# One more pair of the second feed-forward by seven products, with three pairs' weight sums, one unit's low part and a root moved to transfers

## The chip, the cores and the metric

The kernel runs on one core of a Trainium2 chip. Its engines each work through an instruction queue of their own, in order: TensorE (PE, with PEld for its weight loads), VectorE (DVE), ScalarE (ACT), GpSimd (POOL) and SyncE (SP), whose queue (SPq) only issues transfers here. POOL issues transfers too (POOLq), among them all those that add to what already stands at the destination. Semaphores let one engine wait for another. The metric is the device time of one execution in microseconds (us); less is better.

## What is computed

One layer for 512 prompt tokens and 8 single-token decoding sequences, 520 tokens in all, D_MODEL 1024, D_FF 2816. Cut to what matters here:

```python
def rmsnorm(x, g):
    return x * lax.rsqrt(jnp.mean(x * x, axis=-1, keepdims=True) + EPS) * g

def swiglu(x, w_gate, w_up, w_down):
    return (jax.nn.silu(x @ w_gate) * (x @ w_up)) @ w_down

def layer(x, ...):
    x = x + 0.5 * rmsnorm(swiglu(rmsnorm(x, ffn1_pre_g), *ffn1_w), ffn1_post_g)
    h = rmsnorm(x, mix_pre_g)
    ...        # o_r: retention, o_g: gated delta rule, both from h @ w_in
    y = (jax.nn.sigmoid(gate_r) * (o_r @ w_ret_branch)
         + jax.nn.sigmoid(gate_g) * (o_g @ w_gdn_branch))
    x = x + rmsnorm(y @ w_out, mix_post_g)
    return x + 0.5 * rmsnorm(swiglu(rmsnorm(x, ffn2_pre_g), *ffn2_w), ffn2_post_g)
```

All inputs and outputs are float32.

## The kernel before

**Operands.** Activations lie with channels on the 128 partitions and tokens along the free axis, in two halves of 260 tokens. To keep float32 precision every operand is split into a rounded high part and the low rest, and each product runs as three passes per 128 channels (`passes`, L409 to L416): high weights by high activations (L414), high weights by low activations (L415), low weights by high activations (L416). A weight tile arrives as `raw` (512 KB, L276 and L287, two buffers), ACT casts it to `whi` (L355) and DVE subtracts to get `wlo` (L356). A *unit* is one such tile; for 8 blocks of 128 channels, two halves and three passes it takes 48 matmuls.

**The feed-forwards.** Gate and up tiles come in pairs. `PLAIN` says how many pairs at the start are done plainly, as two units of 48 matmuls each: 3 in the first feed-forward, 4 in the second. The others (18 in the second) go by seven products in place of eight of half the depth: 7 products of 12 matmuls, 84 in all (`product7`, matmul tile `sv`). Each of the seven takes a 128 by 512 weight combination, which `split_seven` casts on ACT (L373) and subtracts on DVE (L374). Two combinations are sums that a DMA accumulates: `begin_pair` (L295 to L297) loads the first terms `s3`, `s1` and the plain part `a22` on SP, and `add_sums` (L307) issues two adding transfers on POOL. Two more are worked out on DVE: `s2` (L369) and `s4` (L377). The activation side has combinations too, made once by `token_factors` (L801 to L830): for each of four steps k, DVE works out `xd`, `ta` and twice `tb` (L816 to L820), ACT scales and casts (L815, L818, L824 `th`) and DVE subtracts `tl` twice (L825). The results of the seven products are combined in `pair`: ACT copies one product out of PSUM as `u` (L909), one as `q` (L912) and one as `u` again (L915).

**The way from the mixer to the second feed-forward.** The mixer's last products (`br`) give `branch` its input: DVE multiplies by the gate (L1281), POOL adds the other branch (`bt`, L1282), ACT casts `yh` (L1287) and DVE subtracts `yl` (L1288). Eight `wo` units (`down`, matmul tile `dn`) multiply these. Their results are squared on ACT (`s`, L528) and summed; at the third of them SP issues eight loads of the residual `x` (`load_x`, L743). `post` takes the inverse root of one half after the other (POOL's `rs` 87x3, L471), multiplies on DVE (L645), adds to the residual on POOL (L647) and splits the new residual into `xhl` (L517, L518). The first gate and up units of the second feed-forward (`first_units`, matmul tile `g`) start half by half on these; the first half's results are copied out of PSUM as `early` (L792). While they run, DVE adds the squares (`sq`, L549), PE sums them over channels (`ss`, L477), DVE writes the mean `ms` (L467), POOL takes the inverse root `rs` 87x6 (L471), PE spreads it over all partitions as `rb` (L483, 12 records) and ACT and DVE copy one half each (L573, L571). `hidden` then computes silu of the gate times up for the plain pairs: DVE `t` (L889), ACT `s` (L893), DVE `h` (L896).

**The order.** Every helper is a generator; `tick` runs between groups of matmuls and advances them, and a `yield n` puts the rest n ticks later. The `LATER` table adds or takes ticks at single places. So the code order on each engine's queue is fixed when the kernel is built. `self.rooted` becomes true when the second mean is there, and only then do `token_factors` of the second feed-forward and its `begin_pairs` start.

Of the kernel before, what the change touches and what calls it, by code (L numbers as in the profile page):

```python
# [7 lines left out]
F32 = mybir.dt.float32  # L8
F32R = mybir.dt.float32r
AF = mybir.ActivationFunctionType  # L10
ALU = mybir.AluOpType
# [22 lines left out]
PIECE_AT = [i * (HC - PW) // (PIECES - 1) for i in range(PIECES)]  # L34
# [8 lines left out]
PLAIN = {1: 3, 2: 4}  # L43
SPLIT_H = (8, 21)
LEAD = 3
GATE_COLS = 72
# [124 lines left out]
class Kernel:  # L171
    def __init__(self, ctx, tc, a):
# [34 lines left out]
        self.rooted = False  # L207
        self.ahead = 0
# [58 lines left out]
    def load_to(self, j):  # L267

        nc, a = self.nc, self.a
        while self.raw_next < min(self.group[min(j, len(self.unit_list))] + RAW_BUFS, self.group[-1]):  # L270
            u = self.unit_list[self.first_of[self.raw_next]]
            if u[0] == "seven":
                w, m = a[f"gu{u[1]}"], u[2]
                s1, s3, a22 = self.begun.pop((u[1], m), None) or self.begin_pair(u[1], m)
                t = self.raw.tile([P, KD, P], F32, tag="raw", name=self.name("raw"))
                nc.sync.dma_start(out=t, in_=w[2 * m])  # L276
                t = [t[:, 0:KH], s3, None, a22, t[:, KH:KD], s1, None]
# [64 lines left out]
    def split(self, j, parts):  # L342
# [15 lines left out]
    def split_seven(self, j):  # L358
# [8 lines left out]
        if i == s2:  # L367
# [5 lines left out]
        nc.scalar.copy(w[:, 0], t[i])  # L373
        nc.vector.tensor_tensor(w[:, 1], t[i], w[:, 0].bitcast(F32), ALU.subtract)  # L374
        if i == 4:
# [179 lines left out]
    def inverse_rms(self, acc, r, plus, held=False):  # L555
# [8 lines left out]
        if held:  # L564
            self.hold_sums = False
# [10 lines left out]
        for hf, (c0, n) in enumerate(HALVES):  # L576
            r[hf] = out[:, c0 : c0 + n]
        self.hold_sums = False
# [186 lines left out]
    def first_units(self, xs, name, groups):  # L765
# [4 lines left out]
        early = [self.slot("early") for _ in range(n // 2)]  # L770
        for hf, (c0, cols) in enumerate(HALVES):
            for group in groups:
# [12 lines left out]
                for j in group:  # L785
# [3 lines left out]
                    else:  # L789
# [10 lines left out]

    def token_factors(self, xs, r, gcol, F, f):  # L801

        nc = self.nc
        while len(xs[1]) < KD or f == 2 and not self.rooted:
            yield 0

        if f == 2:
            self.begin_pairs(f)
        tt, stt = nc.vector.tensor_tensor, nc.vector.scalar_tensor_tensor
        for k in range(KH):  # L810
# [9 lines left out]
            stt(out=tb[:, 1], in0=x21, scalar=g2, in1=tb[:, 0], op0=ALU.mult, op1=ALU.subtract)  # L820
            yield 1
# [329 lines left out]
    def mixer(self, xs, r, plus_next, x_from):  # L1151
# [98 lines left out]
        for out, g in ((RG, GR), (GZ, GG)):  # L1250
            for m in range(0, KD, 2):
# [4 lines left out]
                for z in range(2):  # L1256
                    ks = slice(z * H, (z + 1) * H)
                    ps = self.product([((hi[:, ks, :], lo[:, ks, :]), range(H))], ox, "br", z, BRANCH_HALVES)
                    self.spawn(self.branch(g, m + z, gate.pop((g, m + z)), ps, part, yx))
        return self.down(yx, (8,), self.vec[:, V_MPOST : V_MPOST + 8], V_G2PRE, 3, None, plus_next, x_from)  # L1260

    def branch(self, g, m, gate, ps, part, yx):
# [15 lines left out]
        for hf, (c0, n) in enumerate(BRANCH_HALVES):  # L1278
# [3 lines left out]
            nc.gpsimd.tensor_tensor(ts[hf], ts[hf], part[m][:, cs], ALU.add)  # L1282
        yield 3
# [752 lines left out]
```

## Time and profile before

| | |
|---|---|
| median of 3 runs | 1190.89 us (1189.58 to 1191.94) |
| profiled execution | 1189.49 us |
| its span in the profile | 1187.7 us, 1.8 us less than its time |
| granted TensorE clock | 0.999 |
| busy: DVE, ACT, POOL | 907.3, 602.6, 265.2 us |
| matmul and transpose records on PE | 9831 |
| transfers | 170.90 MB, 79178 packets |

Times inside the program are microseconds from the span's start. A timeline row gives the start, the length, the engine, line and operation, result and operands and the number of instructions; an arrow names a releaser: `[0.62 <-ACT yh L1287]` says that the engine stood idle for 0.62 us before this instruction, and that the idle time was ended by ACT's write of `yh` on line 1287. A view by windows gives, for a stretch of time, its length and then the busy time of PE, PEld, DVE, ACT and POOL with the number of instructions in brackets, the granted clock, the share of the DMA engines and the GB/s; asked for PE alone it gives the length, PE, the clock, share and GB/s. The mixer ends near 771 us, the `wo` units run until about 805, and the second feed-forward's first matmul of seven products stands a little after 870.

### The profile page before, as it was taken

To read this page: it belongs to the slowest core of one execution; us is meant where nothing else is said; L and a number is where in the kernel's file an instruction comes from. 1 tells how busy PE (TensorE), PEld (TensorE's weight loads), DVE (VectorE), ACT (ScalarE), POOL (GpSimd) and SP (SyncE) were. 2 spreads that over 40 slices of the span, in tenths; PEclk is the share of its full clock that TensorE was granted. 3 is DMA by queue.
4 is the path that set the end of the run, shared out by engine and by line. 5 is a ranking of instruction groups with operands and counts; after the bars stand their busy time and mean duration, and the time that the engine had idled before them with its cause. 6 is when DMAs were issued, how large, how long until landed. Compare 5 with 4: busy or idle time off the path is not lost. (4 is left out here: it accounts for less than half of the span.)

```text
span 1187.7 us, 25427 instructions
## 1 busy us (share of the span) xinstructions
PE 1172.0 (99%) x9831; PEld 1161.0 (98%) x9831; DVE 907.3 (76%) x1935; ACT 602.6 (51%) x1378; POOL 265.2 (22%) x477
## 2 busy tenths in 40 slices
PE   9999999999999999999999999999999999999998
PEld 8999999999999999999999999999999999999997
DVE  7988888777558788887677777746888888867555
ACT  7656666544336456313354774335555666644331
POOL 1111111000005248755551101404211111000000
PEclk9999999999999999999999999999999999999999
DMA  8777775233342533322367653242677777332334
GB/s 264 186 196 188 183 176 142 70 114 87 109 174 62 179 92 107 105 83 74 111 193 224 225 197 125 76 157 89 178 217 191 185 187 183 103 97 67 98 113 148
DMA packets 79178, 170.90 MB, mean 144 GB/s; under 512 B 17040, under 2 KB 18992, under 8 KB 79056
## 3 DMA queue, kind: packets, MB, share of 16 engines
q1 hardware_dynamic: 66768, 144.98, 38.1%
q0 software_dynamic: 12288, 24.29, 11.9%
q8 instruction: 77, 1.26, 0.4%
q14 instruction: 45, 0.37, 0.1%
HBM read 157.37 MB, written 11.86 MB: 142 GB/s over the span
## 5 line engine op out<-in xcount | busy, mean ns | idle before, releaser
L414 PE MATMUL p<-xhl,whi 128*128 128x260 f32 (+1 forms) x784 | 231.1, 295 | 0.0
L415 PE MATMUL p<-xhl,whi 128*128 128x260 f32 (+1 forms) x784 | 221.3, 282 | 0.1
L416 PE MATMUL p<-xhl,wlo 128*128 128x260 f32 (+1 forms) x784 | 221.2, 282 | 0.0
L356 DVE TENSOR_TENSOR wlo<-raw,whi 128x1024 fp32r<-128x1024 f32 (+2 forms) x111 | 132.9, 1202 | 50.1 <-ACT whi L355 48.4
L414 PE MATMUL sv<-th,w 128*128 128x260 f32 x592 | 167.6, 283 | 1.8 <-ACT q L912 1.8
L415 PE MATMUL sv<-tl,w 128*128 128x260 f32 x592 | 167.1, 282 | 0.0
L416 PE MATMUL sv<-th,w 128*128 128x260 f32 x592 | 167.1, 282 | 0.0
L415 PEld LDWEIGHTS p<-xhl,whi 128*128 128x128 f32 (+1 forms) x784 | 147.2, 188 | 0.7 <-DVE xhl L518 0.7
L414 PEld LDWEIGHTS p<-xhl,whi 128*128 128x128 f32 (+1 forms) x784 | 146.9, 187 | 0.9 <-DVE qk L1562 0.2
L416 PEld LDWEIGHTS p<-xhl,wlo 128*128 128x128 f32 (+1 forms) x784 | 147.0, 187 | 0.0
L307 POOL DMA_DIRECT2D s<-gu_in x74 | 65.0, 954 | 308.4 <-DMA s<-gu_in 156.1
L374 DVE TENSOR_TENSOR w<-s,w 128x512 fp32r<-128x512 f32 x148 | 101.6, 689 | 37.6 <-ACT w L373 36.7
L414 PE MATMUL dn<-hh,whi 128*128 128x260 f32 x448 | 127.0, 283 | 0.0
L415 PE MATMUL dn<-hl,whi 128*128 128x260 f32 x448 | 126.7, 283 | 0.0
L416 PE MATMUL dn<-hh,wlo 128*128 128x260 f32 x448 | 126.6, 283 | 0.0
L355 ACT CAST whi<-raw 128x1024 fp32r<-128x1024 f32 (+2 forms) x111 | 111.0, 1008 | 30.7 <-DMA raw<-dn_in 16.2
L414 PEld LDWEIGHTS sv<-th,w 128*128 128x128 f32 x592 | 111.3, 188 | 2.4 <-ACT q L912 2.2
L415 PEld LDWEIGHTS sv<-tl,w 128*128 128x128 f32 x592 | 111.5, 188 | 0.0
L416 PEld LDWEIGHTS sv<-th,w 128*128 128x128 f32 x592 | 111.4, 188 | 0.0
L373 ACT CAST w<-s 128x512 fp32r<-128x512 f32 x148 | 91.3, 618 | 34.1 <-DVE s L369 23.6
L471 POOL TENSOR_TENSOR rs<-ms,mhalf 87x3 f32<-87x3 f32 (+1 forms) x9 | 11.5, 1281 | 371.2 <-DVE ms L469 309.2
L416 PEld LDWEIGHTS dn<-hh,wlo 128*128 128x128 f32 x448 | 84.4, 188 | 0.0
(436 smaller groups left out, 3444.3 us busy)
## 6 DMA issues: line engine op xcount, KB each, us to landing
raw<-win_in SPq DMA_DIRECT2D x49, 512.0 KB, 3.6
raw<-gu_in SPq DMA_DIRECT2D x48, 512.0 KB, 5.2
s<-gu_in SPq DMA_DIRECT2D x74, 256.0 KB, 5.7
s<-gu_in POOLq DMA_DIRECT2D x74, 256.0 KB, 5.3
raw<-dn_in SPq DMA_DIRECT2D x32, 448.0 KB, 3.4
a<-gu_in SPq DMA_DIRECT2D x37, 256.0 KB, 5.8
x<-x SPq DMA_DIRECT2D x32, 260.0 KB, 5.5
raw<-dn_in SPq DMA_DIRECT2D x16, 512.0 KB, 3.6
```

The lines of the kernel that those rows point to most:

```text
L307: self.nc.gpsimd.dma_start(out=out, in_=term, accum_op=ALU.add)
L355: self.nc.scalar.copy(hi[:, ks], t[:, ks])
L356: self.nc.vector.tensor_tensor(lo[:, ks], t[:, ks], hi[:, ks].bitcast(F32), ALU.subtract)
L373: nc.scalar.copy(w[:, 0], t[i])
L374: nc.vector.tensor_tensor(w[:, 1], t[i], w[:, 0].bitcast(F32), ALU.subtract)
L414: mm(ps, hi[:, k, :], xh, start=first, stop=False, skip_group_check=more)
L415: mm(ps, hi[:, k, :], xl, start=False, stop=False, skip_group_check=more)
L416: mm(ps, lo[:, k, :], xh, start=False, stop=last, skip_group_check=more)
L471: self.nc.gpsimd.tensor_tensor(r[0:PW], m[0:PW], self.mhalf[0:PW].to_broadcast([PW, n]), ALU.pow)
```

## The change

`PLAIN[2]` goes from 4 to 3, so the second feed-forward does 19 pairs by seven products. The first three of these (pairs 3, 4, 5, `WHOLE`) get all four weight sums by transfers: `begin_whole` loads five terms per pair on SP, and `whole_pairs` issues seven adding transfers per pair on POOL, 21 in all, in three rounds (12, 6, 3) after the mixer's last branch. `s2` and `s4` of these pairs are no longer worked out on DVE; as the sums have no negative terms, `s2` is negated in its cast on ACT and in its low part on DVE. One plain unit (5; the table lists 6 and 7 too, which no longer exist) gets its low part without DVE: ACT writes the negated, rounded tile into `wlo` and the cast into `whi`, and a transfer on POOL adds the raw tile from DRAM to `wlo`. The last inverse root is written to DRAM by SP and read back in four broadcast loads (`root_rows`) in place of the `rb` matmuls and copies; with this the three pieces start at tokens 0, 87 and 173. The first units' results are copied out of PSUM for both halves. The first step of the second `token_factors` no longer waits for the mean. The last branch is added on DVE and goes on one tick earlier.

```diff
-PIECE_AT = [i * (HC - PW) // (PIECES - 1) for i in range(PIECES)]
+PIECE_AT = [min(i * PW, HC - PW) for i in range(PIECES)]
...
-PLAIN = {1: 3, 2: 4}
+PLAIN = {1: 3, 2: 3}
+LOW_BY_DMA = {'gu2': (5, 6, 7)}
+WHOLE = 3
...
@@ split
+        kind, m, k0, k1 = self.unit_list[j]
+        if m in LOW_BY_DMA.get(kind, ()):
+            self.nc.scalar.activation(lo, t, AF.Copy, scale=-1.0)
+            self.nc.scalar.copy(hi, t)
+            self.nc.gpsimd.dma_start(out=lo, in_=self.a[kind][m, :, k0:k1, :], accum_op=ALU.add)
+            return
@@ split_seven
+        whole = t[7]
-        if i == s2:
+        if i == s2 and not whole:
             t[s2] = self.slot("s2", (P, KH, P))
...
-        nc.scalar.copy(w[:, 0], t[i])
-        nc.vector.tensor_tensor(w[:, 1], t[i], w[:, 0].bitcast(F32), ALU.subtract)
-        if i == 4:
+        if whole and i == s2:
+            nc.scalar.activation(w[:, 0], t[i], AF.Copy, scale=-1.0)
+            nc.vector.scalar_tensor_tensor(
+                out=w[:, 1], in0=t[i], scalar=-1.0, in1=w[:, 0].bitcast(F32), op0=ALU.mult, op1=ALU.subtract
+            )
+        else:
+            nc.scalar.copy(w[:, 0], t[i])
+            nc.vector.tensor_tensor(w[:, 1], t[i], w[:, 0].bitcast(F32), ALU.subtract)
+        if i == 4 and not whole:
             t[s4] = self.slot("s4", (P, KH, P))
@@ inverse_rms
-        if held:
-            self.hold_sums = False
+        if plus is not None and not held:
+            yield from self.root_rows(s, r)
+            return
+    def root_rows(self, s, r):
+        nc = self.nc
+        n = PIECES * PW
+        yield 2
+        d = self.dram.tile([2 * n], F32, name=self.name("root"))
+        nc.sync.dma_start(out=d.rearrange("(c p) -> p c", p=PW), in_=s[0:PW])
+        yield 3
+        out = self.wk.tile([P, TOK], F32, tag="rb", name=self.name("rb"), bufs=1)
...
+                nc.sync.dma_start(
+                    out=out[:, c0 + t0 : c0 + to], in_=d[hf * n + at : hf * n + at + to - t0].unsqueeze(0).to_broadcast([P, to - t0])
+                )
+        yield 6
@@ first_units
-        early = [self.slot("early") for _ in range(n // 2)]
+        both = name == "g"
+        early = [[self.slot("early") for _ in range(n // 2)] for _ in range(1 + both)]
...
+                if both and hf:
+                    self.prefetch(True, 1)
+                for j in group:
+                    if both or not hf:
                         rows = slice(0, ws[j][0].shape[2])
-                        banks[j][0] = early[j // 2][rows, j % 2 * HC : j % 2 * HC + cols]
-                        self.nc.scalar.copy(banks[j][0], ps[j][rows])
+                        banks[j][hf] = early[hf][j // 2][rows, j % 2 * HC : j % 2 * HC + cols]
+                        self.nc.scalar.copy(banks[j][hf], ps[j][rows])
...
+    def begin_whole(self, f, m, later):
+        dma, w = self.nc.sync.dma_start, self.a[f"gu{f}"]
+        s1, s3, a22, s2, s4 = (self.slot(x, (P, KH, P)) for x in ("s1", "s3", "a22", "s2", "s4"))
+        a11, a12, a21, a4 = (w[2 * m + i, :, k : k + KH] for i in range(2) for k in (0, KH))
+        for out, term in ((s3, a11), (s1, a21), (s2, a11), (s4, a12), (a22, a4)):
+            dma(out=out, in_=term)
+        for out, term in ((s3, a21), (s1, a4), (s2, a21), (s4, a11)):
+            later[0].append((out, term))
+        later[1] += [(s2, a4), (s4, a21)]
+        later[2].append((s4, a4))
+        self.begun[f, m] = s1, s3, a22, s2, s4
+
+    def whole_pairs(self, f):
+        later = [[], [], []]
+        for m in range(PLAIN[f], PLAIN[f] + WHOLE):
+            self.begin_whole(f, m, later)
+            yield 6
+        while not self.joined:
+            yield 0
+        for terms in later:
+            for out, term in terms:
+                self.nc.gpsimd.dma_start(out=out, in_=term, accum_op=ALU.add)
+                yield 1
+            yield 2
...
@@ token_factors
-        while len(xs[1]) < KD or f == 2 and not self.rooted:
+        while len(xs[1]) < KD:
             yield 0
-        if f == 2:
-            self.begin_pairs(f)
...
             stt(out=tb[:, 1], in0=x21, scalar=g2, in1=tb[:, 0], op0=ALU.mult, op1=ALU.subtract)
+            while f == 2 and not self.rooted:
+                yield 0
             yield 1
@@ mixer
+            if out == GZ:
+                self.spawn(self.whole_pairs(2))
...
+        self.joined = True
@@ branch
-            nc.gpsimd.tensor_tensor(ts[hf], ts[hf], part[m][:, cs], ALU.add)
-        yield 3
+            eng = nc.vector if m == KD - 1 else nc.gpsimd
+            eng.tensor_tensor(ts[hf], ts[hf], part[m][:, cs], ALU.add)
+        yield 3 if m < KD - 1 else 2
```

The first place is POOL's queue between the mixer's last additions (`bt`) and the first half's inverse root (`rs` 87x3), before:

```order
L1282 TENSOR_TENSOR bt_10984<-bt_10984,yr_10668 128x256
L1282 TENSOR_TENSOR bt_10984<-bt_10984,yr_10668 128x264
L471 TENSOR_TENSOR rs_11431<-ms_11429,mhalf 87x3
L647 TENSOR_TENSOR x_11099<-x_11099,t_11448 128x260
```

and after, where eight rows stand for the 21 additions: the four of pair 3's first round, its two of the second, and the last round's first and last (a number behind `s_` names one sum):

```order
L1357 TENSOR_TENSOR bt_10969<-bt_10969,yr_10633 128x264
...
L868 DMA s_1820_10663<-gu_in 128x512
L868 DMA s_1819_10662<-gu_in 128x512
L868 DMA s_1822_10665<-gu_in 128x512
L868 DMA s_1823_10666<-gu_in 128x512
...
L868 DMA s_1833_10723<-gu_in 128x512
L868 DMA s_1834_10724<-gu_in 128x512
...
L868 DMA s_1823_10666<-gu_in 128x512
...
L868 DMA s_1849_10791<-gu_in 128x512
L489 TENSOR_TENSOR rs_11482<-ms_11480,mhalf 87x3
```

POOL's last two `bt` additions have left its queue (DVE makes them now), and 21 adding transfers stand between the branch and the inverse root.

The second place is DVE's queue behind the last `xhl` of the residual, before:

```order
L549 TENSOR_TENSOR sq_11496<-sq_11496,sq_11503 128x520
L356 TENSOR_TENSOR wlo_11875<-raw_11601,whi_11874 128x1024
L467 TENSOR_SCALAR ms_11895<-ss_11888 87x6
L561 TENSOR_SCALAR plus_27_155<-ms_11895 87x6
L816 TENSOR_TENSOR xd_11914<-x_11099,x_11103 128x260
L817 SCALAR_TENSOR_TENSOR ta_11912<-x_11103,vec,xd_11914 128x260
L819 SCALAR_TENSOR_TENSOR tb_11913<-x_11099,vec,ta_11912 128x260
L820 SCALAR_TENSOR_TENSOR tb_11913<-x_11101,vec,tb_11913 128x260
```

and after:

```order
L536 SCALAR_TENSOR_TENSOR xhl_11836<-x_11150,vec,xhl_11836 128x260
L885 TENSOR_TENSOR xd_11841<-x_11143,x_11147 128x260
L886 SCALAR_TENSOR_TENSOR ta_11839<-x_11147,vec,xd_11841 128x260
L888 SCALAR_TENSOR_TENSOR tb_11840<-x_11143,vec,ta_11839 128x260
L889 SCALAR_TENSOR_TENSOR tb_11840<-x_11145,vec,tb_11840 128x260
L567 TENSOR_TENSOR sq_11547<-sq_11547,sq_11548 128x520
...
L367 TENSOR_TENSOR wlo_11887<-raw_11654,whi_11886 128x1024
L485 TENSOR_SCALAR ms_11968<-ss_11961 87x6
```

The four operations of `token_factors`' first step have moved from behind the mean to ahead of the seven sums of squares and of unit 4's `wlo`.

The third place is ACT's queue at the first pairs by seven products, where `u` (first product out of PSUM) and `q` (another) are copied and `s` is the silu of a plain pair, before:

```order
L893 ACTIVATE s_12173<-t_12163 128x260
L893 ACTIVATE s_12174<-t_12164 128x260
L373 CAST w_2085_12223<-s_2011_11900 128x512
L373 CAST w_2090_12234<-raw_12060 128x512
L373 CAST w_2093_12289<-s_2015_11907 128x512
L373 CAST w_2094_12292<-s_2077_12160 128x512
L909 COPY u_12301<-sv_12282 128x260
L373 CAST w_2098_12318<-s_2097_12316 128x512
L912 COPY q_12321<-sv_12303 128x260
```

and after:

```order
L391 CAST w_2073_12139<-raw_11949 128x512
L964 ACTIVATE s_12143<-t_12109 128x260
L964 ACTIVATE s_12144<-t_12110 128x260
L964 ACTIVATE s_12168<-t_12157 128x260
L964 ACTIVATE s_12169<-t_12158 128x260
L391 CAST w_2083_12189<-s_1831_10721 128x512
L391 CAST w_2084_12192<-s_1823_10666 128x512
L980 COPY u_12203<-sv_12182 128x260
L386 ACTIVATE w_2087_12219<-s_1833_10723 128x512
L983 COPY q_12222<-sv_12205 128x260
```

Before, one silu pair and four casts stand ahead of the first `u` copy here; after, two silu pairs stand together, the second (`s_12168`, `s_12169`) with two casts between it and the copy.

More of the change, by code (lines that the diff above doesn't have):

```diff
@@ L207, in __init__ @@
         self.rooted = False
+        self.joined = False
         self.ahead = 0
@@ L273, in load_to @@
                 w, m = a[f"gu{u[1]}"], u[2]
-                s1, s3, a22 = self.begun.pop((u[1], m), None) or self.begin_pair(u[1], m)
+                s1, s3, a22, *both = self.begun.pop((u[1], m), None) or self.begin_pair(u[1], m)
                 t = self.raw.tile([P, KD, P], F32, tag="raw", name=self.name("raw"))
                 nc.sync.dma_start(out=t, in_=w[2 * m])
-                t = [t[:, 0:KH], s3, None, a22, t[:, KH:KD], s1, None]
+                t = [t[:, 0:KH], s3, None, a22, t[:, KH:KD], s1, None, bool(both)]
+                if both:
+                    t[2], t[6] = both
             elif u[0] == "down7":
@@ L563, in inverse_rms @@
         self.hold = held
-        if held:
-            self.hold_sums = False
+        if plus is not None and not held:
+            yield from self.root_rows(s, r)
+            return
+        self.hold_sums = False
         yield 4
@@ L577, in inverse_rms @@
             r[hf] = out[:, c0 : c0 + n]
+        self.hold_sums = False
+    def root_rows(self, s, r):
[6 more added lines that the diff above has]
+        out = self.wk.tile([P, TOK], F32, tag="rb", name=self.name("rb"), bufs=1)
+        last = PIECE_AT[-1]
+        for hf, (c0, _) in enumerate(HALVES):
+            for at, to in ((0, last), (n - PW, HC)):
+                t0 = to - (PW if at else last)
+                nc.sync.dma_start(
+                    out=out[:, c0 + t0 : c0 + to], in_=d[hf * n + at : hf * n + at + to - t0].unsqueeze(0).to_broadcast([P, to - t0])
+                )
+        yield 6
+        for hf, (c0, cols) in enumerate(HALVES):
+            r[hf] = out[:, c0 : c0 + cols]
         self.hold_sums = False
@@ L788, in first_units @@
                         self.release()
-                    else:
+                if both and hf:
+                    self.prefetch(True, 1)
+                for j in group:
+                    if both or not hf:
                         rows = slice(0, ws[j][0].shape[2])
-                        banks[j][0] = early[j // 2][rows, j % 2 * HC : j % 2 * HC + cols]
-                        self.nc.scalar.copy(banks[j][0], ps[j][rows])
+                        banks[j][hf] = early[hf][j // 2][rows, j % 2 * HC : j % 2 * HC + cols]
+                        self.nc.scalar.copy(banks[j][hf], ps[j][rows])
                 if hf:
```

## The prediction

> **What bounds the kernel now.** I read the busy table first, then PE alone in a quiet stretch, then PE's waits, and last the timelines around the places that the change touches.
>
> ```profile
> PE 1172.0 (99%) x9831; PEld 1161.0 (98%) x9831; DVE 907.3 (76%) x1935; ACT 602.6 (51%) x1378; POOL 265.2 (22%) x477
> ```
>
> PE is busy all the time, so time goes only where matmuls go or where PE stands. The stretch from 900 to 1000 us (length, PE busy and matmuls, clock, DMA share, GB/s) gives the price of one:
>
> ```profile
> 900.00:1000.00 100.00, 100.00 (x837) 1.00 0.75 187
> ```
>
> 100 us for 837 matmuls at full clock is 0.1195 us each. One pair by seven products in place of two plain units is 84 in place of 96 matmuls: 1.43 us less. The waits of PE (total, times, longest) say what else there is to win near the change:
>
> ```profile
> PE rb L483 <- POOL rs L471: 1.9, 3, 1.0
> PE u L414 <- DVE h L896: 0.5, 1, 0.5
> ```
>
> None is long, and the whole kernel has little idle PE; a change that shortens work on DVE or ACT pays only through such waits. What it can cost is any new wait.
>
> **Part A, the last branch on DVE.** Before, POOL's last additions and PE's wait are:
>
> ```profile
> 772.09 1.44 POOL L1282 TENSOR_TENSOR bt<-bt,yr 128x256 f32<-128x256 f32 x2 [1.33 <-DVE bt L1281]
> 774.05 0.39 PE L414 MATMUL dn<-yh,whi 128*128 128x260 f32 x1 [0.62 <-ACT yh L1287]
> ```
>
> POOL needs 1.44 us for two; DVE's additions of 260 columns take 0.42 (below), so the operand is ready about 0.6 us sooner. Low parts come from DVE right behind, so I take 0.45 of the 0.62: **-0.45 us**.
>
> **Part B, the 21 adding transfers.** POOL is free from 771, and the additions stand in its queue from there. Two stretches show what such transfers do to SP's. From 853 to 859 both queues have work (packets, MB, share of 16 engines); from 864 to 869 SP's alone:
>
> ```profile
> q0 software_dynamic: 381, 0.70, 63.4%
> q1 hardware_dynamic: 365, 0.93, 43.9%
> ```
>
> ```profile
> q1 hardware_dynamic: 1020, 1.90, 99.7%
> ```
>
> Together they fill the engines (107%), and they pass equal numbers of packets: 63 and 61 a us. Alone SP passes 204 a us. So a queue of additions cuts SP to under a third. Between 843 and 876 six additions went through q0 (the last number below is the median time to landing):
>
> ```profile
> q0 software_dynamic: 764, 1.40, 24.2%
> s<-gu_in POOLq DMA_DIRECT2D x6, 256.0 KB, 8.1
> ```
>
> That is 128 packets each, one for a partition, and 24.2% of 33 us over six is 1.33 us of all engines each. So 21 of them are 2688 packets, 42 us at that rate: they reach from 771 to about 809, since before 778 SP has little. Beside them, from the issues on SP:
>
> ```profile
> 778.03 0.33 SPq L287 DMA_DIRECT2D raw<-wo_in  x1
> 778.41 3.75 SPq L743 DMA_DIRECT2D x<-x  x8
> 784.01 0.33 SPq L287 DMA_DIRECT2D raw<-wo_in  x1
> ```
>
> ```profile
> q1 hardware_dynamic: 2018, 5.28, 45.1%
> x<-x SPq DMA_DIRECT2D x8, 260.0 KB, 5.1
> raw<-wo_in SPq DMA_DIRECT2D x3, 512.0 KB, 3.7
> ```
>
> (The second fence is 771 to 805.) The eight `x` loads are 8 x 128 = 1024 packets and a raw weight tile 128. In SP's order the seventh `wo` tile, issued at 784.01, stands behind them: from 778.03 that is 128 + 1024 + 128 = 1280 packets, 21.1 us at 61. The time from the last packet to landing I bound by two small transfers of the stretch 619 to 630, and take the middle, 2.8:
>
> ```profile
> s<-pack SPq DMA_DIRECT2D x8, 8.0 KB, 3.9
> pack<-s SPq DMA_DIRECT2D x4, 16.0 KB, 1.7
> ```
>
> With -0.45 from part A it lands at 778.0 + 21.1 + 2.8 - 0.45 = 801.4, where before such a tile landed 3.7 us (median) after its issue. It is needed here:
>
> ```profile
> 792.93 1.04 ACT L355 CAST whi<-raw 128x1024 fp32r<-128x1024 f32 x1
> 801.07 0.28 PE L414 MATMUL dn<-yh,whi 128*128 128x260 f32 x1
> ```
>
> PE takes the tile at 801.07 - 0.45 = 800.6; its low part, wanted two matmuls later, needs 1.04 us on ACT, 1.22 on DVE (as `wlo` at 840.54 below) and handovers of 0.2, so the tile must land by 798.4. It is **3.0 us** late. Next, the first gate tile can be issued only when this split is done, near 803.7 (before 795.43, when the buffer came free), lands in 3.5 to 6 us, and ACT casts it ahead of the last squares of `dn`. These end between 808.9 and 811.4, against 810.0 on a schedule shifted by 3.0 - 0.45: 0 to 1.4 us. Additions still run, so I take **1.3 us**. B is +4.3.
>
> ```profile
> 809.16 0.86 POOL L471 TENSOR_TENSOR rs<-ms,mhalf 87x3 f32<-87x3 f32 x1 [35.62 <-DVE ms L467]
> ```
>
> The additions stand ahead of this root on POOL; shifted by 4.3 - 0.45 it is wanted at 813, after their end at 809, so it costs nothing. The cover is 4 us. B's bounds: nothing, if the tile still lands by 798.4; 7 to 8, if additions are a fifth slower than q0's row.
>
> [...]
>
> **Part C, from unit 4 to the pairs by seven.** The stretch from unit 4's first matmul to the fourth `sv` product is 32.70 us before:
>
> ```profile
> 842.70:875.40 32.70, 30.83 (x255) 1.00 0.90 272
> ```
>
> After, it holds units 4 and 5 and three `sv` products, and the extra pair stands later. I follow DVE, whose rows are:
>
> ```profile
> 833.62 1.91 DVE L518 SCALAR_TENSOR_TENSOR xhl<-x,vec,xhl 128x260 fp32r<-128x260 f32 x3 [0.32 <-ACT xhl L517]
> 835.45 5.17 DVE L549 TENSOR_TENSOR sq<-sq,sq 128x520 f32<-128x520 f32 x7
> 840.54 1.22 DVE L356 TENSOR_TENSOR wlo<-raw,whi 128x1024 fp32r<-128x1024 f32 x1
> 844.48 0.16 DVE L467 TENSOR_SCALAR ms<-ss 87x6 f32<-87x6 f32 x1 [2.72 <-PE ss L477]
> 850.20 0.42 DVE L816 TENSOR_TENSOR xd<-x,x 128x260 f32<-128x260 f32 x1
> 851.98 0.42 DVE L571 COPY rb<-rb 128x260 f32<-128x260 f32 x1
> 852.32 0.69 DVE L825 TENSOR_TENSOR tl<-ta,th 128x520 fp32r<-128x520 f32 x1
> 853.54 0.42 DVE L889 TENSOR_TENSOR t<-early,rb 128x260 f32<-128x260 f32 x1
> 860.66 0.68 DVE L374 TENSOR_TENSOR w<-raw,w 128x512 fp32r<-128x512 f32 x1
> 861.26 0.68 DVE L374 TENSOR_TENSOR w<-s,w 128x512 fp32r<-128x512 f32 x1
> ```
>
> (All times here are before B's shift, which moves the whole part alike, with A's -0.45.)
> 1. Unit 4's `wlo`: DVE is free at 835.0; four operations of step 0 (850.20 to 851.98, 1.78), the sums 5.09, `wlo` 1.22: ready at 843.1. PE wants it two matmuls after 842.25: it waits **0.6**.
> 2. Unit 4 ran from 842.70 to 850.79 with the spreading matmuls in it; without them 8.09 - 1.25 = **6.84**, by these rows:
>
> ```profile
> 847.28 1.47 PE L483 MATMUL rb<-cst,rs 87*128 87x87 f32 x12
> 848.53 0.37 PE L414 MATMUL g<-xhl,whi 128*128 128x260 f32 x1
> 850.67 0.28 PE L416 MATMUL g<-xhl,wlo 128*128 128x260 f32 x1
> ```
>
> 3. Unit 5: 48 x 0.1195 = **5.74**, ending at 855.4. Its low part comes from the POOL transfer of 512 KB, issued near 837.5 and wanted near 849: the 8.1 us above for 256 KB and 1.33 for as much again end at 847, so it is covered.
> 4. The first `sv` wants the low part of its weights. DVE: `ms` at 844.7, 0.27 for it and its neighbour, two `tl` 1.22, three steps of 1.78 + 1.22 + 0.17 waiting on ACT, two `t` 0.68, the low part 0.60: 857.0. PE waits **1.4** with the handover. The root read through DRAM is covered: `rs` ends near 846.6, two small transfers of 1.7 to 3.9 each make 850 to 854.4, wanted at 855.7.
> 5. Three `sv` products, 12 x 0.1195 each: **4.29**.
> 6. Before the third, its PSUM bank must be freed by ACT's first `u` copy. Ahead of that, on ACT, stand four silus and two casts, and the last two silus wait for DVE's second `t` pair behind seven low parts (7 x 0.605), two `h` and two `t` (0.68 each): 856.4 + 4.2 + 1.4 = 862.0, then on ACT 0.65 + 1.05 + 0.2 to 863.9:
>
> ```profile
> 870.02 0.76 ACT L893 ACTIVATE s<-t 128x260 f32<-128x260 f32 x2 [1.87 <-DVE t L889]
> 871.71 1.14 ACT L373 CAST w<-s 128x512 fp32r<-128x512 f32 x2
> 872.75 0.36 ACT L909 COPY u<-sv 128x260 f32<-128x260 f32 x1
> ```
>
> PE is ready at 859.7: it waits **4.1**. Nothing in this stretch before waited so long; there the copy ran one silu pair later.
>
> The sum is 23.0 in place of 32.70, so -9.7; the extra pair later adds 84 x 0.1195 = +10.04. **C is +0.35**: the 1.43 us of matmuls, the 1.25 of spreading and about two of small waits are eaten by waits 1, 4 and 6.
>
> Other edits I cost at nothing. The four more `early` copies run where ACT is idle (8.53 us ahead of L818):
>
> ```profile
> 845.21 0.51 ACT L818 ACTIVATE ta<-xd,vec 128x260 f32<-128x260 f32 x1 [8.53 <-DVE xd L816]
> ```
>
> Without that gap they would cost 4 x 0.4. The 15 early loads (3.9 MB, some 10 us at the 1.90 MB in 5 us above) are spread among the first `wo` tiles, over 10 us ahead of the first addition; I take nothing. The removed `s2`, `s4` save DVE time that PE doesn't wait for. The pieces at 0, 87, 173 keep twelve `ss` matmuls.
>
> **Sum.** A -0.45, B +4.3, C +0.35: +4.2. The profiled execution takes 1189.49 (span 1187.7, 1.8 around it), so 1193.7; it lies 1.40 below the median of 1190.89. On the median: 1195.1, which I round to **1195.2**.
>
> **The rivals.**
> - *Transfers hidden* (not slower): the seventh `wo` tile lands by 798.4. It decides whether SP keeps at least 1280 packets in 18 us, 71 a us, beside the additions. Then B is nothing and A + C = -0.1: 1190.8. For it: additions wait for each other in rounds two and three, and POOL issues them 1.3 to 1.5 us apart, so there may be gaps; against it: three additions in 6 us already held SP to 61. [...]
> - *Transfers hidden, and no wait for the copy*: as above, and ACT's `u` copy comes in time since DVE takes silu's input earlier than I order it. Without the 4.1 us: 1186.7. Against it: both queues are in order and stand so.
> - *Additions hold the root*: if each takes a fifth longer than q0's row, the last is done near 819, 6 us after the root is wanted. POOL's `rs` then starts late, DVE's `t` behind it and PE's first gate unit: 1200.4 or so. For it: the 8.1 us of the six additions above, against the 5 or 6 us that round two and three would like.
>
> **How the numbers follow.** Chances: forecast 0.60 (1192.5 to 1199, from B's bounds), transfers hidden 0.24 (1189 to 1192.5), no copy wait 0.08, root held 0.08. A measurement of this kernel tells 0.2%, 2.4 us, from no change. Faster (under 1188.5): the third case and a tail of the second, 0.10. Same: most of the second and the forecast's lower edge, 0.22. Slower: 0.68. The range from 1189.5 to 1200 leaves out the third case, half the fourth and tails, 0.2 in all.
>
> **What would show it.** Part B: PE's `dn` waiting for `wlo` or `whi` near 800 with a releaser ACT or DVE behind a late raw tile, and `x` loads landing after 12 us or more in place of 5.1. Root: a POOL row of `rs` 87x3 whose releaser is POOL's own queue means the fourth case. Part C: waits of PE on `g` (0.6), the first `sv` on DVE's low part (1.4) and on ACT's `u` (4.1). If `dn` doesn't wait, B is wrong; if `sv` doesn't wait for `u`, step 6 is wrong; if the rows in the 900 to 1000 stretch hold fewer matmuls than 837, the extra pair has put a new wait into the steady part, which I haven't priced.

## The result and the profile after

The kernel after takes 1205.47 us (median of 4 runs, 1205.02 to 1206.33), the kernel before 1191.41 us (4 runs, 1189.58 to 1192.23): ratio 1.0121, 95% interval 1.0103 to 1.0139. It is slower by 14 us, where the prediction said 4. The profiled execution took 1205.02 us, its span 1203.3, at a granted clock of 0.994 in place of 0.999.

The busy table and the longest waits of PE, from the page and the waits of the kernel after (waited for, total, times, longest):

```profile
PE 1176.9 (98%) x9807; PEld 1164.7 (97%) x9807; DVE 907.6 (75%) x1939; ACT 608.2 (51%) x1390; POOL 281.0 (23%) x493
```

```profile
PE dn L432 <- ACT whi L366: 6.1, 1, 6.1
PE sv L434 <- DVE w L392: 3.5, 1, 3.5
PE sv L432 <- ACT u L980: 2.4, 1, 2.4
```

The three waits are the ones that the prediction named, at 3.0, 1.4 and 4.1 us (`dn` is a product of the `wo` units, `sv` one of the products by seven). PE has fewer matmuls than before and yet a longer busy time. Where that comes from shows in a view by windows (PE alone: length, busy, clock, DMA share, GB/s):

```profile
790.00:800.00 10.00, 10.00 (x86) 1.00 1.10 262
...
805.00:810.00 5.00, 2.31 (x9) 0.56 1.13 234
...
870.00:875.00 5.00, 4.18 (x22) 0.66 0.29 56
875.00:880.00 5.00, 3.46 (x19) 0.73 1.04 393
...
900.00:1000.00 100.00, 100.00 (x834) 1.00 0.73 182
```

Behind each of the three waits the granted clock drops; the kernel before reads 1.00 over 600 to 900. From 900 to 1000 PE is busy for all 100 us and waits for nothing, as before. That 834 records stand there and not 837 is thus no new wait of the extra pair, which the prediction had made a sign of being wrong. The timeline of PE shows it matmul by matmul:

```profile
800.87 0.28 PE L434 MATMUL dn<-yh,wlo 128*128 128x260 f32 x1
807.23 0.58 PE L432 MATMUL dn<-yh,whi 128*128 128x260 f32 x1 [6.08 <-ACT whi L366]
807.61 0.42 PE L433 MATMUL dn<-yl,whi 128*128 128x260 f32 x1
808.49 0.58 PE L434 MATMUL dn<-yh,wlo 128*128 128x260 f32 x1 [0.46 <-DVE wlo L367]
808.87 0.42 PE L432 MATMUL dn<-yh,whi 128*128 128x260 f32 x1
809.09 0.42 PE L433 MATMUL dn<-yl,whi 128*128 128x260 f32 x1
...
812.52 0.28 PE L434 MATMUL dn<-yh,wlo 128*128 128x260 f32 x1
```

From 808.87 to 812.34 the starts lie 0.22 us apart in place of 0.12: 3.5 us at half speed, some 1.7 us lost, behind a wait of 6.08. In all, 21 matmuls start from 800.87 to 812.52, which is 11.65 us in place of 2.5: 6.5 us of it are the two waits, the other 2.6 the slow clock with the first slow matmuls behind each wait.

Behind the third wait the clock is full at first and drops 0.85 us later:

```profile
876.54 0.39 PE L432 MATMUL sv<-th,w 128*128 128x260 f32 x1 [2.35 <-ACT u L980]
876.76 0.28 PE L433 MATMUL sv<-tl,w 128*128 128x260 f32 x1
...
877.39 0.42 PE L432 MATMUL sv<-th,w 128*128 128x260 f32 x1
```

Three points of the program tell where the time went (start of unit 4, start of the fourth `sv` product, end of the span). Unit 4 starts at 852.27 in place of 842.70: **+9.6**. From there to the fourth `sv`, at 878.69, it is 26.42 in place of 32.70, and with 10.04 for the extra pair **+3.8**. The rest of the program takes **2.3** more: some 0.9 of it is slow clock behind the third wait, most of the rest waits of 0.4 and 0.2 us for operands of later `dn` products (`hp`, `u`) and their neighbours. Unrounded (9.57, 3.76, 2.27) they make 15.6, the difference of the spans.

The transfers of the first stretch, 771 to 812 (queue: packets, MB, share; then transfers, KB, median us to landing):

```profile
q0 software_dynamic: 2906, 5.30, 71.6%
q1 hardware_dynamic: 1861, 4.72, 35.5%
...
s<-gu_in POOLq DMA_DIRECT2D x21, 256.0 KB, 12.3
x<-x SPq DMA_DIRECT2D x8, 260.0 KB, 13.7
raw<-wo_in SPq DMA_DIRECT2D x3, 512.0 KB, 16.8
```

An `x` load takes 13.7 us in place of 5.1 and a `wo` tile 16.8 in place of 3.7. The timelines of SP, ACT and POOL give the seventh `wo` tile and the root behind the additions:

```profile
778.41 9.11 SPq L784 DMA_DIRECT2D x<-x  x8
789.29 2.41 SPq L292 DMA_DIRECT2D raw<-wo_in  x2
```

```profile
806.14 1.04 ACT L366 CAST whi<-raw 128x1024 fp32r<-128x1024 f32 x1 [13.15 <-DMA raw<-wo_in]
```

```profile
808.81 0.86 POOL L868 DMA_DIRECT2D s<-gu_in  x1 [4.03 <-DMA s<-gu_in]
818.63 0.88 POOL L489 TENSOR_TENSOR rs<-ms,mhalf 87x3 f32<-87x3 f32 x1 [8.96 <-DVE ms L485]
```

SP needs 9.11 us to issue eight loads (before 3.75), so the tile is issued only at 789.29 (before 784.01), and it lands at 806.1, forecast 801.4. POOL issues the last addition at 808.81; it lands 6.5 us later, at 815.3, where the prediction had the end of all additions at 809. POOL stands 8.96 us until the mean comes: the additions did not hold the root.

Last, the way of the second root:

```profile
855.09 2.87 POOL L489 TENSOR_TENSOR rs<-ms,mhalf 87x6 f32<-87x6 f32 x1 [5.10 <-DVE ms L485]
```

```profile
857.98 0.30 SPq L606 DMA_DIRECT2D root<-rs  x1
863.62 1.76 SPq L613 DMA_DIRECT2D rb<-root  x4
```

```profile
867.58 0.43 DVE L960 TENSOR_TENSOR t<-early,rb 128x260 f32<-128x260 f32 x1 [1.62 <-DMA rb<-root]
868.67 0.43 DVE L960 TENSOR_TENSOR t<-early,rb 128x260 f32<-128x260 f32 x1 [0.66 <-DMA rb<-root]
869.02 0.68 DVE L392 TENSOR_TENSOR w<-raw,w 128x512 fp32r<-128x512 f32 x1
```

The root is on its way from 855.09 to 868.6: 13.5 us. DVE stands 2.28 us for it, and the first low part that PE wants stands behind these two `t`.

### The profile page after: what moved, and what is told of

It is laid out like the page before. It is cut to its first block, busy times and chain, and to the rows that moved or that the text cites. A ratio compares the mean times of both kernels' runs of the same rounds, so it can differ in the third digit from the quotient of the medians.

```text
span 1203.3 us, 25436 instructions
## 1 busy us (share of the span) xinstructions
PE 1176.9 (98%) x9807; PEld 1164.7 (97%) x9807; DVE 907.6 (75%) x1939; ACT 608.2 (51%) x1390; POOL 281.0 (23%) x493
## 5 line engine op out<-in xcount | busy, mean ns | idle before, releaser
L367 DVE TENSOR_TENSOR wlo<-raw,whi 128x1024 fp32r<-128x1024 f32 (+2 forms) x108 | 129.2, 1200 | 67.1 <-ACT whi L366 65.6
L432 PE MATMUL sv<-th,w 128*128 128x260 f32 x608 | 173.7, 286 | 3.6 <-ACT u L980 2.4
L433 PE MATMUL sv<-tl,w 128*128 128x260 f32 x608 | 173.0, 285 | 0.0
L434 PE MATMUL sv<-th,w 128*128 128x260 f32 x608 | 172.6, 284 | 0.0
L312 POOL DMA_DIRECT2D s<-gu_in x70 | 61.5, 956 | 314.1 <-DMA s<-gu_in 223.4
L366 ACT CAST whi<-raw 128x1024 fp32r<-128x1024 f32 (+2 forms) x108 | 108.1, 1007 | 50.6 <-DMA raw<-dn_in 16.9
L432 PEld LDWEIGHTS sv<-th,w 128*128 128x128 f32 x608 | 115.7, 190 | 4.2 <-ACT u L980 2.7
L433 PEld LDWEIGHTS sv<-tl,w 128*128 128x128 f32 x608 | 115.9, 191 | 0.0
L434 PEld LDWEIGHTS sv<-th,w 128*128 128x128 f32 x608 | 115.9, 191 | 0.0
```

Source lines behind the costliest of these rows:

```text
L312: self.nc.gpsimd.dma_start(out=out, in_=term, accum_op=ALU.add)
L366: self.nc.scalar.copy(hi[:, ks], t[:, ks])
L367: self.nc.vector.tensor_tensor(lo[:, ks], t[:, ks], hi[:, ks].bitcast(F32), ALU.subtract)
L432: mm(ps, hi[:, k, :], xh, start=first, stop=False, skip_group_check=more)
L433: mm(ps, hi[:, k, :], xl, start=False, stop=False, skip_group_check=more)
L434: mm(ps, lo[:, k, :], xh, start=False, stop=last, skip_group_check=more)
```

## The experiments

Each run is compared with runs of the kernel before on the same chip (medians 1190.8 to 1191.6). The first four start from the kernel after, or before, and take one thing at a time.

**x loads later.** The edit is one number:

```diff
-            if d == 2 and x_from is not None:
+            if d == 4 and x_from is not None:
```

> The kernel after, with the eight loads of x issued at the fifth wo unit in place of the third, so that the seventh wo tile stands ahead of them on SP's queue. Theory (the 21 additions take more than half of the DMA engines' packets, so what stands behind the x loads comes late, PE stands 6.1 us and then runs at a lower granted clock for some 3.5 us): the wait of PE on whi near 801 falls from 6.1 us to under 0.5, the matmuls after it keep their 0.12 us, and the time falls by 8 to 9.5 us, to 1196 to 1197.5. Rival (the additions hold any tile of SP's up, whatever its place): the seventh tile still lands after 800 and PE still stands for 3 us or more; or the x loads themselves come late for the additions to x near 812 and PE stands there for about as long: 1203 to 1206.

1207.56 us, ratio 1.0131 (1.0111 to 1.0150): a miss, above the ranges of the theory and of the rival. The wait on the `wo` tile is gone, as the theory has it, but not the time: another wait of 9.1 us, which neither had named, took its place. PE's longest wait of this run, and ACT's row behind it:

```profile
PE ss L495 <- DVE acc L547: 9.3, 2, 9.1
```

```profile
813.63 1.04 ACT L366 CAST whi<-raw 128x1024 fp32r<-128x1024 f32 x1 [12.49 <-DMA raw<-gu_in]
```

Now the first gate tile stands behind the `x` loads and lands after 813; ACT casts it in order ahead of the last squares, and their sum comes late. So moving the `x` loads only chose who is late: in both orders it is what stands behind them.

**No additions.** The 21 issues are left out; the kernel leaves the weight sums of three pairs at their first terms, so its output is not the layer's.

> The kernel after without the 21 adding transfers of the first three pairs: their weight sums hold only the first terms, so these three pairs' part of the second feed-forward is left wrong in value; all instructions else stay. Theory: the stretch from 771 to 805 has a DMA share near 0.45 again, x loads land in about 5 us, PE doesn't stand on whi, and 9.5 us go: 1195.5 to 1196.5; what lies behind 850 stays (waits of 3.5 and 2.4 us on the first sv products). Rival (the new order on SP and the 15 early loads make the tile late, not the additions): the wait of 6.1 us stays and the time stays within 1 us of 1205.5.

1195.95 us, ratio 1.0041 (1.0026 to 1.0056): 9.5 us less, as expected. The transfers from 771 to 805 are those of the kernel before again:

```profile
x<-x SPq DMA_DIRECT2D x8, 260.0 KB, 5.2
raw<-wo_in SPq DMA_DIRECT2D x4, 512.0 KB, 3.6
```

Unit 4 starts at 843.30, 0.6 us later than before: so little do the 15 early loads and the order on SP cost, and the additions cost the other 9.0 of the 9.6. What stays are waits of 3.6 and 1.7 us at the first `sv` products. Behind both the clock is half (0.42 us a matmul, as in the slow stretches of the kernel after, where full clock shows 0.28), from 861 to 873.6 with the waits between; the second wait found it half already:

```profile
867.74 0.59 PE L432 MATMUL sv<-th,w 128*128 128x260 f32 x1 [1.65 <-ACT u L979]
868.12 0.42 PE L433 MATMUL sv<-tl,w 128*128 128x260 f32 x1
```

**Root by matmuls.** `inverse_rms` goes on to its `rb` matmuls and copies, as before, and never to `root_rows`.

> The kernel after with the last inverse root spread by matmuls and two copies as in the kernel before, in place of the way through DRAM. Theory (the root's way through DRAM took 13 us, and DVE's two t, which need it, stand ahead of the first low part of the pairs' weights, so PE's wait of 3.46 us is the root's): that wait falls to 1.4 us or less and the slow clock behind it goes, PE gets 1.25 us of spreading matmuls back, the wait for the u copy may grow towards 4.1 us: a net of 1 to 3 us less, 1202.5 to 1204.5. Rival (DVE would be late with the low part anyway, since its own chain of factors ends near 866): the wait stays near 3 us and the time grows by about 1.3 us, to 1206.8.

1203.94 us, ratio 1.0098 (1.0081 to 1.0115), 1.5 less than after and within the range expected. The wait on the low part went, so it was the root's, and the one for the `u` copy fell to 0.9 us, where the theory let it grow; but 2.8 us on `th`, the factors' cast on ACT, came, again with slow clock soon behind it (the granted clock of the run is 0.994, as after). Removing one wait let another show. The wait on the `wo` tile stays, at 5.6.

**Stalls in the kernel before.** The edit, in short:

```diff
             self.product7(SEVEN, F, "sv", banks, i)
             at(i)
+            if plain == PLAIN[2] and n in (42, 63, 84):
+                self.stall(banks, {42: 2, 63: 8, 84: 16}[n])
...
+    def stall(self, banks, k):
+        src = next(x for x in banks if x is not None)
...
+        self.nc.scalar.copy(t, src[:, 0:PW])
+        for _ in range(k):
+            self.nc.scalar.copy(t, t)
+        ps = self.bank("st")
+        self.nc.tensor.matmul(ps[0:PW, 0:1], t, self.ones[:, 0:1], start=True, stop=True)
```

> The kernel before with three waits put in between pairs of the second feed-forward, far from the change: after the 43rd, 64th and 85th product by seven, ACT copies a piece of the product 3, 9 and 17 times, and one small matmul needs the last copy. All else is computed as before. Theory (a long enough wait of PE is followed by matmuls at half the granted clock): waits of some 1, 2.5 and 4.5 us; behind the longer two the pitch goes from 0.12 to 0.22 us for 15 to 18 matmuls, 1.5 to 1.8 us lost each; behind the first perhaps none; the time grows by the waits plus about 3.5 us. Rival (the slow clock of the kernel after came from its transfers, not its waits): the pitch stays 0.12 behind all three, and the time grows by the waits alone, about 8 us.

1203.15 us (2 runs), ratio 1.0096 (1.0074 to 1.0118). The three places in PE's timeline:

```profile
936.12 0.32 PE L1084 MATMUL st<-ones,st 128*87 128x1 f32 x2 [1.19 <-ACT st L1082]
...
969.72 0.31 PE L1084 MATMUL st<-ones,st 128*87 128x1 f32 x2 [2.96 <-ACT st L1082]
...
970.10 0.28 PE L415 MATMUL sv<-xhl,w 128*128 128x260 f32 x1
970.22 0.28 PE L416 MATMUL sv<-xhl,w 128*128 128x260 f32 x1
...
1005.67 0.45 PE L1084 MATMUL st<-ones,st 128*87 128x1 f32 x2 [5.32 <-ACT st L1082]
...
1006.56 0.42 PE L416 MATMUL sv<-xhl,w 128*128 128x260 f32 x1
1006.78 0.42 PE L414 MATMUL sv<-xhl,w 128*128 128x260 f32 x1
```

Waits of 1.19 and 2.96 us leave the pitch at 0.12; behind 5.32 it is 0.22 until 1009.4. So a wait alone, with no transfers added, brings the slow clock; but only one of the two longer ones did, where the theory had both. The price is not simply a function of the length: in the kernel after, the shorter wait of 2.35 us had slow clock behind it. In the profiled runs, waits of up to 1.65 us that PE met at full clock left it full (the longest is one with the `x` loads later), 2.35 us was followed by slow clock, 2.96 was not, and every one of 3.0 us or more was. The slow stretches hold from 12 matmuls (behind the first wait with six additions) to 26 (behind the second without additions), which is some 1.2 to 2.6 us more at 0.10 us each.

In the kernel after the granted clock reads 0.50 from 808.87 to 812.34 and from 870.65 to 873.90, and 0.51 from 877.40 to 880.80: 3.5, 3.3 and 3.4 us. In the run without additions one slow stretch lasts 5.9 us.

**The silu of the plain pairs later.** Two weight tiles are prepared ahead of the last step of the factors, and `leads` waits four ticks behind the root:

```diff
             def leads():
+                while r[0] is None or r[1] is None:
+                    yield 0
+                yield 4
                 for j in range(0, len(lead), 2):
...
+            elif f == 2 and k == KH - 2:
+                self.prefetch(True, 2)
             yield 2
```

> The kernel after with the queues of DVE and ACT reordered where the pairs by seven begin: the casts and low parts of the first two weight tiles stand ahead of the last step of the token factors, and the silu of the plain pairs starts four ticks after the root is there, behind the first low parts and the u copy. Theory (PE's waits of 3.5 and 2.4 us come from what stands ahead in these two queues, and the slow clock behind them from the waits): both waits fall under 1 us, the pitch stays 0.12, 7 to 9 us go: 1196.5 to 1198.5. Rival (DVE has too much work there in any order, as in the run with the root by matmuls, where a wait for the factors took the place of the other): PE waits 2.5 us or more on factors (th, tl) and still runs slow behind it: 1202 to 1205.5.

1200.05 us, ratio 1.0076 (1.0061 to 1.0092): 5.4 us less, short of the 7 to 9. The wait on the low part went; the one on the `u` copy is 3.0, with slow clock behind it (starts 0.22 us apart in two stretches of 2.2 us from 871.14 to 876.45). The first half of the theory held, the second did not. The wait on the `wo` tile is 5.6 here too.

**Six additions.** The first three pairs get `s3` and `s1` by transfers only; DVE works out `s2` and `s4` between the products again. The early loads go from 15 to 9 with it.

```diff
...
-        for out, term in ((s3, a11), (s1, a21), (s2, a11), (s4, a12), (a22, a4)):
+        for out, term in ((s3, a11), (s1, a21), (a22, a4)):
             dma(out=out, in_=term)
-        for out, term in ((s3, a21), (s1, a4), (s2, a21), (s4, a11)):
+        for out, term in ((s3, a21), (s1, a4)):
             later[0].append((out, term))
-        later[1] += [(s2, a4), (s4, a21)]
-        later[2].append((s4, a4))
-        self.begun[f, m] = s1, s3, a22, s2, s4
+        self.begun[f, m] = s1, s3, a22
```

> The kernel after with six additions in place of 21 and nine early loads in place of 15: the first three pairs get two sums by transfers (as the later pairs do) and DVE works out the other two. Theory (it is the amount of additions beside the x loads and the seventh wo tile): 6 x 1.33 us of transfers are over by about 780, the tile lands before 798 and PE doesn't stand on it: 9 us less in that stretch; DVE has two more sums per pair, up to 1 us more behind 865: 1196 to 1198. Rival (already the first additions, which SP's transfers queue behind, make the x loads late): PE still stands 2 us or more at 801 and its clock drops: 1200 to 1203.

1197.79 us, ratio 1.0055 (1.0041 to 1.0069), as expected. PE no longer stands on the `wo` tile: the amount of additions decided (the last two runs below have all 15 loads beside six additions, and no such wait either). The wait on the low part stays at 3.6 us, and with the sums on DVE the one for the `u` copy is 4.5.

**Both.**

> Both edits at once: the reordered queues and six additions. If the two theories hold and their effects add, 16 to 18 us go: 1187.5 to 1189.5, which is faster than the kernel before by 1.5 to 4 us. Rival (the sums that DVE works out again stand in its queue where the low parts of the first pair are wanted): PE waits 1.5 us or more on low parts of the third and later products: 1190.5 to 1193.

1194.06 us (11 runs), ratio 1.0022 (1.0014 to 1.0031). A miss: 11.4 us less than after, where the two runs alone gave 5.4 and 7.7 and 16 to 18 were expected. One wait of 5.0 us on the `u` copy is left, not one on low parts as the rival had it. ACT's queue there:

```profile
862.75 1.24 ACT L391 CAST w<-s 128x512 fp32r<-128x512 f32 x2
864.88 0.76 ACT L964 ACTIVATE s<-t 128x260 f32<-128x260 f32 x2 [0.88 <-DVE t L960]
865.54 0.36 ACT L980 COPY u<-sv 128x260 f32<-128x260 f32 x1
```

The copy still stands behind seven casts and a silu that waits for DVE.

**The copies first, and the silu last.** The edit on top of both:

```diff
...
             self.product7(SEVEN, F, "sv", banks, i)
             at(i)
+            if plain == PLAIN[2] and x_from is not self.a["xT"] and n < 6:
+                self.prefetch(True, 2)
+                self.hold_sums = n < 5
```

with 16 ticks for `leads` in the first run, 30 in the second.

> The kernel with six additions and reordered queues, with two more changes of order: up to the sixth product by seven only two weight tiles are cast at a time, each time behind the copy of the product just made, and the silu of the plain pairs starts 16 ticks after the root. Theory (the 5.0 us wait that is left comes from the u copy standing on ACT behind seven casts and a silu pair that waits for DVE): that wait falls under 1 us, the slow clock behind it goes, 5 to 7 us less than the 1194.1 of that kernel: 1187 to 1189, which beats the kernel before by 2 to 4 us. Rival (DVE, with the sums back in its queue, is itself too late there): PE waits on low parts or factors for as long, 1191 to 1194.

> As the run with the copies first, with the silu of the two first plain pairs 30 ticks after the root in place of 16, so that DVE and ACT have less to do while the first two pairs by seven run. If DVE's queue still sets the pace there, 0.5 to 2 us less than that run; if not, the same within 0.5 us.

1194.38 us, ratio 1.0029 (1.0017 to 1.0041), and 1193.91 us, ratio 1.0028 (1.0019 to 1.0036). A miss for the first: the `u` copy's wait of 5.0 us fell to 1.1, but another of 3.9 us came some products later. It stands on DVE, as the rival had it, though not on low parts or factors: on DVE's `v`, which must read a PSUM bank before PE may fill it again. With the silu at 30 ticks it is 3.2 us. The times are the same within 0.5 us, which the second expectation had made the sign that DVE's queue does not set the pace. So these two runs show that order alone moves the wait, and leave open whether it is the amount of DVE's work.

**The root through DRAM without the rest.** Four plain pairs, no whole pairs, no `LOW_BY_DMA`, `begin_pairs` after the mean as before.

> The kernel after with three of its edits taken back: four plain pairs as before, no whole pairs, no low part by a transfer. What is left of the change is the root through DRAM, the first units' copies for both halves, the token factors' first step ahead of the mean, the pieces' places and the last branch on DVE. Theory (each of these is worth only the 1.25 us of spreading matmuls and the waits of 0.53 and 0.36 us on rb, and the way through DRAM, 12 us long, is hidden behind two more plain units of 5.74 us each): no wait over 1.3 us appears and the time is 1 to 2.5 us below before: 1188.5 to 1190. Rival (the root by DRAM is late here too, since silu's input stands ahead of the first weights' low part on DVE): a wait of 2 us or more on w or u near 870 with a slow clock behind it, 1192 to 1195.

1199.78 us, ratio 1.0073 (1.0056 to 1.0089). A clear miss, in the rival's direction and beyond its size: one wait of 12.0 us on the first `sv`, for DVE's `t`. PE's wait, SP and DVE in this run:

```profile
PE sv L432 <- DVE t L962: 12.0, 1, 12.0
```

```profile
849.65 0.54 SPq L606 DMA_DIRECT2D root<-rs  x1
863.46 2.74 SPq L613 DMA_DIRECT2D rb<-root  x4
```

```profile
867.42 0.43 DVE L962 TENSOR_TENSOR t<-early,rb 128x260 f32<-128x260 f32 x1 [5.97 <-DMA rb<-root]
870.82 0.43 DVE L962 TENSOR_TENSOR t<-early,rb 128x260 f32<-128x260 f32 x1 [2.97 <-DMA rb<-root]
```

The 2 KB of the root take 13.8 us before the loads may start, where six weight loads were issued just ahead of them on SP's queue and four additions behind on POOL's; in the kernel after, with two weight tiles just ahead, 5.6. So the way through DRAM has no fixed price: it was longer where more transfers stood around it. Whether the loads or the additions made it so was not tried apart.

**The sums early.** From the run with the silu last: 15 loads as after, six additions on POOL, and 20 ticks behind them DVE finishes the sums where it is half idle:

```diff
-        later[1] += [(s2, a4), (s4, a21)]
-        later[2].append((s4, a4))
+        later[1] += [(s2, s1), (s4, s2)]
...
+        for out, term in later[1]:
+            self.nc.vector.tensor_tensor(out, out, term, ALU.add)
+            yield 1
```

> As the run with the silu last (19 pairs, six additions on POOL), with the 15 early loads of the kernel after, and the other two sums of the three first pairs made by six DVE additions some 20 us after the mixer, where DVE is half idle, in place of subtractions between the first products. Theory (in the runs with reordered queues DVE's amount of work from 847 to 873 sets PE's wait of 3.2 to 3.9 us there, two sums a pair and the handovers to ACT between a sum and its low part with it): the wait falls under 1.2 us, no slow clock behind it, 3 to 5 us less than 1193.9: 1189 to 1191. Rival (the wait comes from the place of single operations, such as the q and v steps, and not from the amount): a wait of 2.5 us or more stays there, 1192.5 to 1194.

1190.60 us (11 runs), ratio 0.9993 (0.9983 to 1.0003), as expected, and no change from before. The longest waits of PE behind the mixer:

```profile
PE sv L432 <- ACT w L391: 1.2, 1, 1.2
PE sv L432 <- ACT u L988: 1.1, 1, 1.1
```

No slow clock is left there: behind each of the two only the first start is late (0.20 and 0.23 us to the next), then they lie 0.12 us apart, and the granted clock of the run is 0.999 where the kernel after has 0.994. Taking work away between the root and the second pair did what order had not. How much of it is DVE's time and how much the handovers to ACT between a sum and its low part is not separated.

**The silu at 90 ticks.** On top of the sums early.

> As the run with the sums made early, with the silu of the first two plain pairs 90 ticks after the root in place of 30, when weight tiles are cast well ahead again. Theory (the waits of 0.6 and 1.2 us that stand at 882 and 886 in that run come from these silus and from nothing else): both fall under 0.3 us, 1.2 to 1.7 us less than 1190.6: 1189 to 1189.5, faster than the kernel before by 2 us. Rival (they come from the sums of the fourth pair, which DVE makes there again): the waits stay or move by a few us, 1190 to 1191.

1190.16 us (11 runs), ratio 0.9990 (0.9981 to 0.9999). The waits at 882 and 886 went, and waits of 1.4 and 0.6 us came at 928 and 933; one of 1.2 us stays near 870. The time is in the rival's range, above the 1189 to 1189.5 expected. It is the lowest median of all versions, 0.1% under the kernel before, with an interval that just leaves out no change; against the run before it (0.9990 and 0.9993) the difference is not shown.

## Why the prediction was wrong

- **The sign and the places were right, the size was not.** The prediction had 1195.2 with a range to 1200.0; 1205.47 lies above it. All three new waits were named, with their releasers. The spans differ by 15.6 us where the sum gave 4.2, so 11.4 us are missing from it.
- **What failed first: each new wait was priced by its length alone**, and the clock was left out. The matmuls at 0.22 us behind them cost some 1.7 us behind the first (3.5 us at half speed), 1.5 behind the second (870.65 to 873.9) and 1.6 behind the third (877.4 to 880.8): nearly 5 of the 11.4 us, and with the first slow matmuls behind the first wait nearly 6. Every row quoted from before had a clock of 1.00, so none of them could show it; the run with stalls does.
- **Part A was -0.45 and is -0.05.** POOL's addition was replaced by one in DVE's own queue between two gate multiplications, so the last `yh` came as late: PE starts at 774.00 (before 774.05) and 774.47 (before 774.51).
- **Part B, the term of the `wo` tile, was mis-sized: 3.0 for 6.1 us, or 6.5 with the 0.46 for its low part.** The rate was nearly right (q0 and q1 share packets evenly: 355 and 351 from 796 to 801, 70 a us each where 61 was taken). The count and the start were not. From 776 to 781 q0 alone passed 549 packets and SP none, though the sixth `wo` tile and the `x` loads were issued at 778. SP's first packets pass at 782, near the end of the thirteen additions that POOL issues without a pause, from 770.90 to 782.56. And each transfer brings 16 small packets of its own (before, 224 under 512 B in the 14 transfers of 771 to 805), so 1280 should be 1440. The 1.3 us for the first gate tile did not come, since PE was then late enough itself: it stood 0.18 us on the squares' sum. The additions not holding the root was right, with 8.96 us of room.
- **Part C, step 1**, the wait of 0.6 for unit 4's low part, is 0.51. **Step 4** was wrong in one clause: "the root read through DRAM is covered". `rs` took 2.87 us in place of 1.58 before, the write 5.6 and the read 3.5, where 1.7 to 3.9 were taken each; the root was there at 868.6, and the first low part, ready for DVE at 865.9 without it, waited with the `t` ahead of it: 3.46 in place of 1.4. **Step 6** named the right wait with the right queue; as the step before took longer, part of its 4.1 had passed: 2.35. The two together are 5.8 for 5.5. Steps 2 and 3 hold; step 5 counts the matmuls rightly but has them all at 0.1195 us.
- **The rivals.** "Transfers hidden" is ruled out by the tile's landing at 806.1, and the run without additions shows that they made it late; "no copy wait" is ruled out by the wait of 2.35 us, and "root held" by POOL's row. The largest rival was none of them: that a wait costs more than its length.
- **What stays open.** Why SP's transfers passed nothing for some 4 us (778 to 782) behind queued additions, and what decides whether a wait of 2.3 to 3 us brings the slow clock, is not shown here. Why `rs` on 87x6 took 2.87 us wasn't tried. That the gain of 1.43 us of matmuls and 1.25 of spreading shows only as 1 us in the best version may lie in the waits of 0.5 to 1.4 us that its timeline still has; this wasn't taken apart.

## What to carry to other kernels

Before work goes from an engine to transfers, count the packets of all queues in the stretch, the small ones included, and ask what stands behind them on the other queue; moving a load may only choose who is late. Where TensorE is the bound, a wait can cost more than its length: here one of 2.35 us already had slow clock behind it, for some 1.2 to 2.6 us more a time, while waits of up to 1.65 us at full clock had none. And where an engine's queue is full just behind a join, move its work to a stretch where it idles (here six additions of 0.69 us) rather than reorder it or give it to transfers.

## What the runs showed of the hardware

An addition of 256 KB by transfer holds the DMA engines 1.47 us before (four from 845 to 868: 576 packets, 25.6% of 23 us) and, with 21 in a row, 1.45 us (770 to 818: 3024 packets, 63.6% of 48 us). The prediction's 1.33 came from a stretch in which 764 of the 864 packets of six passed. A 2 KB write to DRAM with the read behind it was there after 9.1 to 10.6 us in the kernel after and after 17.8 to 21.2 us among six weight loads and four additions.
